# Diagonal recurrence of a third mixer: states in pairs, outputs in fours, small products alternating between row and column groups

## The chip, the cores and the metric

The kernel runs on one core of one Trainium2 chip. TensorE (PE) multiplies matrices, VectorE (DVE) and ScalarE (ACT) work elementwise, GpSimd (POOL) does almost nothing here, and the queue of SyncE (SP) issues the transfers from the chip's memory. All engines run their own instruction lists in order and wait for each other by semaphores. The metric is the time of one execution on the device in microseconds (us); the kernel before was timed three times.

## The reference: what is computed

A stack of layers over 256 tokens of width 1024: two blocks (a state space scan with neighbourhood attention, then an mLSTM, each with a feed-forward part) and then a third block. The third block's mixer adds up three branches of width 512: a gated attention ("fox"), a diagonal complex recurrence (S5), and a gated linear recurrence (HGRN2). Behind it come attention over a memory and a gated feed-forward part. The change touches the S5 branch alone:

```
def s5_mixer(u, a_re, a_im, b_re, b_im, c_re, c_im, d_skip, log_dt, w_glu, b_glu):
    ug = uf.reshape(bsz, seq, S5_GROUPS, S5_GROUP)
...
    drive_r = jnp.einsum('bsgh,gph->bsgp', ug, bbar_r)
    drive_i = jnp.einsum('bsgh,gph->bsgp', ug, bbar_i)
...
    _, _, h_r, h_i = lax.associative_scan(_complex_linear_combine, elems, axis=1)
    y = (jnp.einsum('bsgp,ghp->bsgh', h_r, c_re.astype(f32))
         - jnp.einsum('bsgp,ghp->bsgh', h_i, c_im.astype(f32)))
    y = y.reshape(bsz, seq, S5_W) + d_skip.astype(f32) * uf
    z = jax.nn.gelu(y)
    out = z * jax.nn.sigmoid(z @ w_glu.astype(f32) + b_glu.astype(f32))
```

## The kernel before, in words

The program is one long list of large products on PE. A weight unit (128 x 2048 numbers, `unit`, transfer at L437) is taken in two halves of 128 x 1024; ACT copies each half to its high part `wh` (L350) and DVE subtracts to get the low part `wl` (L359), and PE makes three products for each piece of weight (high by high, high by low, low by high; below: full products, 128 x 128 by 128 x 256 tokens). A unit is 48 of them. `wh` and `wl` have four buffers each, the raw weights three. The large sums lie in PSUM banks of the pool `mm`, the small ones in banks of the pool `ax`.

The third mixer (phase "mixer2") goes through its projections in the order `M2_ORDER = "su fox hz hv g2 g0 b0 glu dr g1 b1 b2"`. `su` makes the S5 input (two tiles `su` of 128 channels x 2 x 256 tokens) and then puts the generator `s5()` (L1357) into a list of background work. Between the units of large products the program calls `tick`, which takes a step or so of the other chains (fox, HGRN2) and of the background. A scheduler may then still move instructions within each engine.

The 2048 complex states are 16 blocks j of 128, and each block belongs to 32 of the 512 channels. One step of `s5()` handles one block: it loads a table of cosines and sines (`s5tl`), makes two drives on PE (`ax<-su,s5bt`: 32 rows of channels, from row 32 (j mod 4), to 128 states by 256 tokens, real and imaginary part into one `ax` bank), and then ten DVE instructions turn the drive by the table (two products, two half-sized sums), scan the two parts over the tokens with the state's magnitude, and turn back (two products). The work tiles are `s5w1` and `s5w2`; the trace shows both as `s5w`. One step later, by `lagged`, four products (`ax<-s5w,s5c`: 128 states to 32 partitions, from partition 32 (j mod 4), by 256 tokens) give the block's output; after each fourth block a DVE instruction adds the sum to `su`. These small products are in full float32, and the trace lists each as two passes (two rows each).

When all blocks are done, `s5()` ends with the gelu of `su`, and the unit `glu` multiplies it by its weights (`s5_gate`).

Of the kernel before, what the change touches and what calls it, by code (L numbers as in the profile page):

```python
# [19 lines left out]
P = 128  # L20
# [6 lines left out]
# order of the steps of the first mixer (x, z, q/k/v of attention; b: further background) and of the third one  # L27
# [3 lines left out]
# heads of the memory's keys and values that are projected at the ends of the layers' parts  # L31
FILLERS = [("k0 k1", "mm"), ("v0 v1", "ax"), ("k2 k3", "mm"), ("v2 v3", "ax")]
# units of the gated feed-forward that are computed by tokens first, and how many of them wait for their transposes
# [12 lines left out]
# ---------------------------------------------------------------- layout of the inputs  # L46
# [33 lines left out]
# the projections of the third mixer: name, first column, number of columns  # L80
# [11 lines left out]
def _units(w):  # L92
    """[1024, 256 m] -> m units [128, 8 * 256]"""
    m = w.shape[1] // T
    return w.reshape(8, P, m, T).transpose(2, 1, 0, 3).reshape(m, P, 2048)


def _down(w):
    """[256 m, 1024] -> m units [128, 2 * 1024]"""
    m = w.shape[0] // T  # L100
    return w.reshape(m, 2, P, D).transpose(0, 2, 1, 3).reshape(m, P, 2048)


def _square(w):
    """[512, 512 m] -> m units [128, 4 * 512]"""
    m = w.shape[1] // 512
    return w.reshape(4, P, m, 512).transpose(2, 1, 0, 3).reshape(m, P, 2048)
# [13 lines left out]
def prepare(i):  # L121
# [114 lines left out]
    # neighbourhood bias: entry (row distance, column distance), NEG outside of the window  # L236
# [29 lines left out]
# ---------------------------------------------------------------- the program  # L266

class Stack:
# [31 lines left out]
    # ---- small helpers  # L300
# [5 lines left out]
    def phase(self, name, mm=4, apart=(), swap=False):  # L306
        """tiles that live within one phase of the program; mm of the eight banks are for the large products;
        apart: tags with pools of their own, so that they lie where the neighbouring phases leave room in time"""
# [65 lines left out]
    # ---- steps of a chain that are put between the units of the large products  # L374
# [3 lines left out]
    def tick(self, n=1, background=1):  # L378
        """n steps of the chains in order (a chain that yields True waits for others), some of the background's
        (fractions add up)"""  # L380
# [22 lines left out]
    def held(self, on=True):  # L403
        """what is traced here is issued after the norm that ended the last phase"""
# [5 lines left out]
    def lagged(self, steps):  # L410
        """generator: each step's second part after the next one's first part"""
# [17 lines left out]
    # ---- weights: a unit is [128, 2048], taken as high and low parts in two halves  # L429
# [24 lines left out]
    def small_unit(self, name):  # L454
        """generator: a few columns for all inputs, in pieces of 512 of a tile's columns"""
# [11 lines left out]
    def proj_tok(self, u, xh, xl, kind="mm", after=False):  # L467
        """256 columns of x @ W -> [128 tokens, 2, 256]; after: behind the last phase's products, returns also
        the last product"""
# [12 lines left out]
    def proj_feat(self, u, xh, xl):  # L482
        """256 columns of x @ W -> [128 features, 2, 256 tokens]"""
# [11 lines left out]
    def proj_blocks(self, units, rows):  # L495
        """generator: as proj_feat for some units and proj_rows for one small one (rows: name, PSUM), two blocks of 128
        inputs at a time; the sums of one bank are one group, opened by the first product"""
# [24 lines left out]
    def proj_half(self, u, yh, yl):  # L522
        """512 columns of y [512 features] @ W -> two tiles [128 features, 2, 256 tokens]"""
# [14 lines left out]
    def down(self, units, acc, first, last):  # L538
        """acc[t][c] += y @ W with 256 rows of W each (units: (u, yh, yl), y [128, 2, 256]), one half
        of the tokens after the other"""  # L540
# [15 lines left out]
    def out_units(self, name, ys, order, tick=0, tail=2, early=0):  # L556
        """accumulators of y @ W; ys[j] is filled by the chains"""
# [23 lines left out]
    # ---- 1/sqrt(v*inv + eps) to float32 accuracy: a first guess from the exponent, then a  # L581
    # polynomial in v*guess^2 (its leading coefficient folded into the scale of v)
# [19 lines left out]
    # ---- split of a float32 value into two float32r parts (src may be in PSUM)  # L602
# [4 lines left out]
    def first_norm(self):  # L607
        """generator: rms norm of x, transposed, and the modulation of the first mixer (shift and scale), two
        blocks of 128 features at a time; scaled and shifted -> self.xh, self.xl"""
# [54 lines left out]
    def rms(self, x, xn):  # L664
        """1 / root mean square of the rows of x (xn: room for the squares)"""
# [39 lines left out]
    # ---- modulation: sums over the 1024 inputs of silu(c) * ada_w  # L705
# [9 lines left out]
    def cond_first(self, out):  # L715
        """silu(c) along the row on every partition, kept in DRAM"""
# [7 lines left out]
    def cond_row(self, out):  # L724
        """silu(c) along the row, on every partition"""
# [3 lines left out]
    def ada(self, layer, chunks, G=None, kind="ax"):  # L729
        """generator: a[.], b[.] columns of both norms and the rows of both gates"""  # L730
# [43 lines left out]
    # ---- x += G * rmsnorm(acc), or x += acc; then the norm of the next block  # L774
# [25 lines left out]
    # ---- layer 1 and 2: feed-forward  # L800
# [27 lines left out]
    # ---- softplus(v) and log_sigmoid(v)  # L828
# [12 lines left out]
    # ---- keys and values of the memory  # L841
    def mem_norm(self):
        """the normalised memory (features on partitions), kept in DRAM"""
# [17 lines left out]
    def mem_fill(self, what, kind, mh, ml):  # L861
        """keys (k) or values (v) of some heads, kept in DRAM, right behind the last phase's products; the first
# [494 lines left out]
    def s5(self, us):  # L1357
# [10 lines left out]
        def step(j):  # L1368
# [6 lines left out]
            for c in range(2):  # L1375
                self.matmul(dp[:, c], bt[b:b + 32, c, f], u[b:b + 32])
# [527 lines left out]
```

## Time and profile before

| | |
|---|---|
| time, median of 3 runs | 1548.85 us (1548.67 to 1549.3) |
| profiled execution, first to last instruction (span) | 1547.9 us; its time outside the span is not given |
| busy: PE, DVE, ACT, POOL | 96%, 75%, 55%, 0% of the span |
| mean granted clock of PE | 0.996 of full speed |
| third mixer's S5, first drive to the first product of `glu` | about 977.6 to 1194.9 us |

Busy shares are means over stages with different limits, so the stretch of S5 is read by itself. "Granted clock" is the share of full speed that the profile shows for PE in a stretch; 1.00 is 2.4 GHz and 0.50 is 1.2 GHz. The small products lie scattered among the large ones, so a reader looks for them by their tiles.

### The profile page before, as it was taken

How to read it: one execution, taken by the hardware profiler on the slowest of the kernel's cores; microseconds unless marked ns; L12 is line 12 of the kernel's file. 1: busy time of each engine (PE TensorE's matmuls, PEld its weight loads, DVE VectorE, ACT ScalarE, POOL GpSimd, SP SyncE). 2: the span in 40 equal slices, each digit the busy share in tenths (PEclk: the TensorE clock that was granted, in tenths of full speed). 3: DMA queues.
4: the chain of work that ended last, by engine and by line, in shares of the span. 5: the costliest groups of instructions: out<-in, count | busy, mean ns of one | idle time of the engine just before them, and what ended most of it. 6: DMA issues, size and time to landing. Idle time of an engine off the chain costs nothing.

```text
span 1547.9 us, 25416 instructions
## 1 busy us (share of the span) xinstructions
PE 1488.8 (96%) x9964; PEld 1325.5 (86%) x9964; DVE 1166.1 (75%) x2223; ACT 855.9 (55%) x1502; POOL 4.5 (0%) x26
## 2 busy tenths in 40 slices
PE   2899999999999989999999999999999999999999
PEld 2878887898898889998889989877789999799998
DVE  8788878877778896667988866858888987565555
ACT  4776765654546555554756765445444456454443
POOL 0000000000000000000000000000000000000000
PEclk9999999999999999999999999989999999999999
DMA  9656777577886785446576665323343355235552
GB/s 351 236 136 190 267 280 265 199 300 275 327 298 224 269 296 190 142 160 204 221 268 230 236 227 191 126 93 112 127 157 109 134 208 204 109 137 191 184 178 101
DMA packets 62058, 315.47 MB, mean 204 GB/s; under 512 B 6385, under 2 KB 15217, under 8 KB 28146
## 3 DMA queue, kind: packets, MB, share of 16 engines
q1 hardware_dynamic: 61938, 313.85, 57.5%
q8 instruction: 78, 1.28, 0.3%
q14 instruction: 42, 0.34, 0.1%
HBM read 304.77 MB, written 9.05 MB: 203 GB/s over the span
## 4 chain that ended last, share of the span: by engine, by line
PE 80%; DVE 11%; DMA 4%; ACT 3%; issue 2%; SPq 0%; ACTq 0%; DVEq 0%
PE mm L365 51%; PE ax L365 26%; DVE wl L359 2%; PE ax L369 2%; DMA bp<-cs_d 1%; DMA raw<-in_ada 1%; DVE acc L750 1%; ACT xn L350 1%; ACT wh L350 1%; DVE acc L637 1%; DMA bp<-nM_d 1%; DVE cva L362 0%; DVE qt L359 0%; DMA nb<-in_nab 0%; PE mm L369 0%
## 5 line engine op out<-in xcount | busy, mean ns | idle before, releaser
L359 DVE TENSOR_TENSOR wl<-raw,wh 128x1024 fp32r<-128x1024 f32 x400 | 485.5, 1222 | 202.2 <-ACT wh L350 201.6
L350 ACT ACTIVATE wh<-raw 128x1024 fp32r<-128x1024 f32 x400 | 419.5, 1057 | 369.3 <-PE mm L365 208.5
L365 PE MATMUL mm<-xh,wh 128*128 128x256 f32 x1536 | 441.3, 287 | 3.8 <-ACT bp L350 2.8
L365 PE MATMUL mm<-xh,wl 128*128 128x256 f32 x1536 | 439.3, 286 | 0.5 <-DVE wl L359 0.4
L365 PE MATMUL mm<-xl,wh 128*128 128x256 f32 x1536 | 439.4, 286 | 0.0
L365 PEld LDWEIGHTS mm<-xh,wh 128*128 128x128 f32 x1536 | 296.5, 193 | 13.8 <-issue 6.8
L365 PEld LDWEIGHTS mm<-xl,wh 128*128 128x128 f32 x1536 | 296.6, 193 | 7.8 <-issue 6.0
L365 PEld LDWEIGHTS mm<-xh,wl 128*128 128x128 f32 x1536 | 296.4, 193 | 5.3 <-issue 3.6
L365 PE MATMUL mm<-wh,xh 128*128 128x256 f32 x496 | 143.3, 289 | 0.0
L365 PE MATMUL mm<-wl,xh 128*128 128x256 f32 x496 | 141.8, 286 | 0.3 <-DVE wl L359 0.2
L365 PE MATMUL mm<-wh,xl 128*128 128x256 f32 x496 | 141.2, 285 | 0.0
L365 PE MATMUL ax<-wh,mhh 128*128 128x512 f32 x256 | 102.4, 400 | 0.0
L365 PE MATMUL ax<-wl,mhh 128*128 128x512 f32 x256 | 101.3, 396 | 0.0
L365 PE MATMUL ax<-wh,mhl 128*128 128x512 f32 x256 | 101.3, 396 | 0.0
L365 PEld LDWEIGHTS mm<-wl,xh 128*128 128x128 f32 x496 | 94.9, 191 | 3.4 <-issue 2.3
L365 PEld LDWEIGHTS mm<-wh,xh 128*128 128x128 f32 x496 | 94.8, 191 | 3.0 <-issue 2.5
L365 PEld LDWEIGHTS mm<-wh,xl 128*128 128x128 f32 x496 | 94.9, 191 | 1.6 <-issue 1.5
L365 PEld LDWEIGHTS ax<-wh,mhl 128*128 128x128 f32 x256 | 48.1, 188 | 12.0 <-DVE mhl L359 0.4
L365 PEld LDWEIGHTS ax<-wh,mhh 128*128 128x128 f32 x256 | 48.2, 188 | 10.7 <-ACT wh L350 0.5
L365 PEld LDWEIGHTS ax<-wl,mhh 128*128 128x128 f32 x256 | 48.1, 188 | 10.7 <-issue 0.5
L362 DVE SCALAR_TENSOR_TENSOR acc<-raw,cond,acc 128x1024 f32<-128x1024 f32 x28 | 35.8, 1278 | 9.3 <-DMA raw<-in_ada 9.1
L750 DVE CUSTOM_DVE_ANT_0 acc<-raw,crow 128x1024 f32<-128x1024 f32 x32 | 39.0, 1219 | 2.4 <-DMA raw<-in_ada 2.1
(486 smaller groups left out, 2601.4 us busy)
## 6 DMA issues: line engine op xcount, KB each, us to landing
raw<-in_wts SPq DMA_DIRECT2D x214, 1024.0 KB, 4.9
raw<-in_ada SPq DMA_DIRECT2D x48, 1024.0 KB, 6.0
nb<-in_nab SPq DMA_DIRECT2D x16, 256.0 KB, 2.9
grow<-in_rows SPq DMA_DIRECT2D x16, 256.0 KB, 5.1
bp<-cs_d SPq DMA_DIRECT2D x16, 256.0 KB, 6.2
s5tab<-s5t SPq DMA_DIRECT2D x16, 256.0 KB, 2.5
s5tl<-s5tab SPq DMA_DIRECT2D x16, 256.0 KB, 2.9
meml<-mem_d SPq DMA_DIRECT2D x2, 1024.0 KB, 6.2
```

Of the source, the lines that this page charges most:

```text
L350: return self.nc.scalar.activation(out=out, in_=in_, func=func, **kw)
L359: return self.nc.vector.tensor_tensor(out=out, in0=in0, in1=in1, op=op)
L362: return self.nc.vector.scalar_tensor_tensor(out=out, in0=in0, scalar=s, in1=in1, op0=op0, op1=op1)
L365: return self.nc.tensor.matmul(out, lhsT, rhs, start=start, stop=stop)
L369: return self.nc.tensor.transpose(out, in_, self.ident[0:k, 0:k])
L637: nc.vector.tensor_tensor_reduce(out=acc, in0=raw[:, k * D:(k + 1) * D], in1=self.crow, scale=1.0, scalar=0.0, op0=ALU.mult, op1=ALU.add, ...
L750: nc.vector.tensor_tensor_reduce(out=acc, in0=w, in1=self.crow, scale=1.0, scalar=0.0, op0=ALU.mult, op1=ALU.add, accum_out=s8[:, j:j + 1])
```

## The change

`s5()` now takes the blocks in pairs. A step p loads two tables, takes two `ax` banks, and issues the four drives of its two blocks so that neighbouring products use different groups of 32 rows (block 2p+1, then 2p, for the real part, and again for the imaginary part). The DVE work of both blocks follows, with the same ten instructions for each. After every second pair, `outputs(f)` makes all sixteen output products of four blocks at once, in an order where neighbouring products write different groups of 32 partitions. A helper `after` adds dependencies of issue order alone, so that all of a group come behind its first. The first work tile of a block now lies in the space of `merged0` to `merged3` (each used later for the merged branches), the second in four buffers of `s5w2`; the gelu uses `s5w2` too. The pool `mm` has four of the eight PSUM banks in this phase instead of five, `ax` four instead of three. The rest of the diff (left out here) removes comments.

```
+    def after(self, first, later):
+        if first is None:
+            return later
+        self.order(later, first)
+        return first
...
-        def step(j):
-            b, f = 32 * (j % 4), j // 4
+        held = []
+
+        def step(p):
+            f = p // 2
             u = us[f // 2][:, f % 2]
-            tab = self.pt("s5tl", [P, 2, T], bufs=2)
-            nc.sync.dma_start(out=tab, in_=self.s5tab[j].rearrange("p (a b) -> p a b", a=2))
-            co, si = tab[:, 0], tab[:, 1]
-            dp = self.ax((P, 2, T))
+            js = (2 * p, 2 * p + 1)
+            tabs, dps = [], []
+            for j in js:
+                tab = self.pt("s5tl", [P, 2, T], bufs=2)
+                nc.sync.dma_start(out=tab, in_=self.s5tab[j].rearrange("p (a b) -> p a b", a=2))
+                tabs.append(tab)
+                dps.append(self.ax((P, 2, T)))
+            first = None
             for c in range(2):
-                self.matmul(dp[:, c], bt[b:b + 32, c, f], u[b:b + 32])
-            w1 = self.pt("s5w1", [P, 2, T], bufs=2)
-            w2 = self.pt("s5w2", [P, 2, T], bufs=2)
...
-            def rest():
-                if j % 4 == 0:
-                    yps.append(self.ax((P, 512))[:, 0:T])
-                yp = yps[-1]
-                # C_re (re cos - im sin) - C_im (re sin + im cos)
-                for i, (c, w) in enumerate(((0, w2[:, 0]), (2, w1[:, 1]), (1, w1[:, 0]), (1, w2[:, 1]))):
-                    self.matmul(yp[b:b + 32], cc[:, c, j], w, i == 0, i == 3)
-                if j % 4 == 3:
-                    self.stt(u, u, self.col("s5d", f), yp, ALU.mult, ALU.add)
-            return rest
-
-        yield from self.lagged([partial(step, j) for j in range(16)])
+                for j, dp in zip(js[::-1], dps[::-1]):
+                    b = 32 * (j % 4)
+                    first = self.after(first, self.matmul(dp[:, c], bt[b:b + 32, c, f], u[b:b + 32]))
+            for j, tab, dp in zip(js, tabs, dps):
+                w1 = self.pt(f"merged{j % 4}", [P, 2, T])
+                w2 = self.pt("s5w2", [P, 2, T], bufs=4)
...
+                held.append((j, w1, w2))
+
+        def outputs(f):
+            u = us[f // 2][:, f % 2]
+            yp = self.ax((P, 512))[:, 0:T]
+            first = None
+            for i in range(4):
+                for j, w1, w2 in held[::-1]:
+                    b = 32 * (j % 4)
+                    c, w = ((0, w2[:, 0]), (2, w1[:, 1]), (1, w1[:, 0]), (1, w2[:, 1]))[i]
+                    first = self.after(first, self.matmul(yp[b:b + 32], cc[:, c, j], w, i == 0, i == 3))
+            held.clear()
+            self.stt(u, u, self.col("s5d", f), yp, ALU.mult, ALU.add)
+
+        for p in range(8):
+            step(p)
+            yield
+            if p % 2:
+                outputs(p // 2)
+            yield
...
-            a = self.pt("s5w1" if i == 0 else "s5w2", [P, 2, T], bufs=2)
+            a = self.pt("s5w2", [P, 2, T], bufs=4)
...
-    with S.phase("mixer2", 5, LATE2):
+    with S.phase("mixer2", 4, LATE2):
```

What follows shows the order of instructions on two engines; the numbers behind the names tell apart the tiles of one tag. On PE before, near the end of S5, the drives of block 15 and the outputs of block 14 stand together between two full products (`mm`):

```order
L365 MATMUL mm_12284<-xh_9998,wl_12292 128x256
L365 MATMUL ax_12347<-su1_10393,s5bt_10561 128x256 x2
L365 MATMUL ax_12192<-s5w2_12271,s5c_10563 32x256
L365 MATMUL ax_12192<-s5w1_12270,s5c_10563 32x256 x2
L365 MATMUL ax_12192<-s5w2_12271,s5c_10563 32x256
L365 MATMUL mm_12364<-xh_9998,wh_12367 128x256
```

The same engine after the change has the four drives of a pair (p = 6, blocks 12 and 13) between two full products:

```order
L365 MATMUL mm_12015<-xh_9998,wl_12023 128x256
L365 MATMUL ax_12102<-su1_10393,s5bt_10561 128x256
L365 MATMUL ax_12099<-su1_10393,s5bt_10561 128x256
L365 MATMUL ax_12102<-su1_10393,s5bt_10561 128x256
L365 MATMUL ax_12099<-su1_10393,s5bt_10561 128x256
L365 MATMUL mm_12127<-xh_9998,wh_12130 128x256
```

And the last outputs of the changed kernel, `outputs(3)`, stand on PE with blocks 15, 14, 13 and 12 in turn (the first eight of sixteen products, and the full product ahead of them):

```order
L365 MATMUL mm_12369<-xl_9999,wh_12372 128x256
L365 MATMUL ax_12351<-s5w2_12281,s5c_10563 32x256
L365 MATMUL ax_12351<-s5w2_12271,s5c_10563 32x256
L365 MATMUL ax_12351<-s5w2_12118,s5c_10563 32x256
L365 MATMUL ax_12351<-s5w2_12108,s5c_10563 32x256
L365 MATMUL ax_12351<-merged3_12280,s5c_10563 32x256
L365 MATMUL ax_12351<-merged2_12270,s5c_10563 32x256
L365 MATMUL ax_12351<-merged1_12117,s5c_10563 32x256
L365 MATMUL ax_12351<-merged0_12107,s5c_10563 32x256
```

Two products that stood next to each other before used the same rows and columns of the array; now neighbours differ in them. In the changed order the drives stand in 12 runs (five pairs whole, p = 2 and 5 broken up by products of fox, p = 7 in two halves with 34 full products between them), and the sixteen outputs of the four calls in 8 (one whole, two broken once, one twice). Between the last drives of a pair and the outputs that need it stand, on PE: 111 full products and then the transposes of `qksq` (p = 1), 72 full products (p = 3), 64 (p = 5), and 64 to the first product that needs the split described next (p = 7).

On DVE before, at the end of S5, the work on block 14 is mixed with splits of weights (`wl`):

```order
L359 TENSOR_TENSOR wl_12368<-raw_12365,wh_12367 128x1024
L359 TENSOR_TENSOR s5w1_12270<-ax_12267,s5tl_12265 128x512
L359 TENSOR_TENSOR s5w2_12271<-ax_12267,s5tl_12265 128x512
L359 TENSOR_TENSOR wl_12372<-raw_12365,wh_12371 128x1024
L359 TENSOR_TENSOR s5w1_12270<-s5w1_12270,s5w2_12271 128x256 x2
L372 SCALAR_TENSOR_TENSOR s5w2_12271<-mag_8452,s5w1_12270 128x256 x2
L359 TENSOR_TENSOR s5w1_12270<-s5w2_12271,s5tl_12265 128x512
L359 TENSOR_TENSOR s5w2_12271<-s5w2_12271,s5tl_12265 128x512
L359 TENSOR_TENSOR wl_12446<-raw_12443,wh_12445 128x1024
```

After the change, blocks 14 and 15 (p = 7) stand there interleaved, behind three splits in a row, and the split `wl_12377` of a unit still to be multiplied comes behind most of them:

```order
L359 TENSOR_TENSOR merged2_12270<-ax_12262,s5tl_12260 128x512
L359 TENSOR_TENSOR s5w2_12271<-ax_12262,s5tl_12260 128x512
L359 TENSOR_TENSOR merged3_12280<-ax_12265,s5tl_12263 128x512
L359 TENSOR_TENSOR merged2_12270<-merged2_12270,s5w2_12271 128x256 x2
L359 TENSOR_TENSOR s5w2_12281<-ax_12265,s5tl_12263 128x512
L372 SCALAR_TENSOR_TENSOR s5w2_12271<-mag_8452,merged2_12270 128x256 x2
L359 TENSOR_TENSOR merged3_12280<-merged3_12280,s5w2_12281 128x256
L359 TENSOR_TENSOR merged2_12270<-s5w2_12271,s5tl_12260 128x512
L359 TENSOR_TENSOR merged3_12280<-merged3_12280,s5w2_12281 128x256
L359 TENSOR_TENSOR s5w2_12271<-s5w2_12271,s5tl_12260 128x512
L372 SCALAR_TENSOR_TENSOR s5w2_12281<-mag_8452,merged3_12280 128x256 x2
L359 TENSOR_TENSOR wl_12377<-raw_12370,wh_12376 128x1024
```

Where before one split stood between pieces of a single block's chain, now a chain of two blocks stands ahead of it.

## Rows read from the trace of the kernel before

**Rows 1.** The page: busy time of each engine; the chain that ended last.

```profile
PE 1488.8 (96%) x9964; PEld 1325.5 (86%) x9964; DVE 1166.1 (75%) x2223; ACT 855.9 (55%) x1502; POOL 4.5 (0%) x26
...
PE 80%; DVE 11%; DMA 4%; ACT 3%; issue 2%; SPq 0%; ACTq 0%; DVEq 0%
```

**Rows 2.** What PE waited for, 950 to 1250: us in total, times, longest.

```profile
PE ax L365 <- DVE s5w L359: 0.2, 1, 0.2
```

**Rows 3.** S5's stretch: us, busy (x) of PE, PEld, DVE, ACT, POOL; PEclk, DMA, GB/s.

```profile
978.70:1194.90 216.20, 215.00 (x1408) 173.90 (x1408) 170.81 (x324) 95.20 (x159) 1.08 (x2) 0.98 0.34 116
```

**Rows 4.** Passes and loads by tile: ns least/median/most, first and last start, shapes.

```profile
L365 PE MATMUL ax<-su,s5bt x64: 374/374/478, 977.6 to 1162.3; 32*128 32x256 f32 x64
...
L365 PEld LDWEIGHTS ax<-s5w,s5c x128: 106/110/110, 989.9 to 1181.0; 128*32 128x32 f32 x128
L365 PE MATMUL ax<-s5w,s5c x128: 379/379/404, 989.9 to 1181.3; 128*32 128x256 f32 x128
```

**Rows 5.** Timeline of PE around one block: start, duration, instruction.

```profile
1161.35 0.28 PE L365 MATMUL mm<-xh,wl 128*128 128x256 f32 x1
1161.56 1.12 PE L365 MATMUL ax<-su,s5bt 32*128 32x256 f32 x4
1162.61 1.91 PE L365 MATMUL ax<-s5w,s5c 128*32 128x256 f32 x8
1164.46 0.39 PE L365 MATMUL mm<-xh,wh 128*128 128x256 f32 x1
1164.68 0.28 PE L365 MATMUL mm<-xl,wh 128*128 128x256 f32 x1
```

**Rows 6.** Timeline of PE, three places with small products of different row or column groups.

```profile
95.08 1.14 PE L365 MATMUL ax<-nk,nq 64*128 64x256 f32 x8
...
108.89 1.09 PE L365 MATMUL ax<-qt,xt 128*64 128x256 f32 x8
...
1016.61 0.48 PE L365 MATMUL ax<-fr,cst 32*128 32x256 f32 x1
1016.61 0.48 PE L365 MATMUL ax<-su,s5bt 32*128 32x256 f32 x1
1016.92 0.37 PE L365 MATMUL ax<-fr,cst 32*128 32x256 f32 x1
```

**Rows 7.** DVE's groups, 975 to 1195: busy us, mean ns | idle before.

```profile
L359 DVE TENSOR_TENSOR wl<-raw,wh 128x1024 fp32r<-128x1024 f32 x43 | 52.2, 1219 | 9.4 <-ACT wh L350 9.4
...
L359 DVE TENSOR_TENSOR s5w<-ax,s5tl 128x512 f32<-128x512 f32 x32 | 20.8, 684 | 7.6 <-PE ax L365 7.5
L372 DVE TENSOR_TENSOR_SCAN s5w<-mag,s5w 128x256 f32<-128x256 f32 x32 | 20.3, 675 | 0.1
```

**Rows 8.** Timeline of DVE within one block: start, duration, instruction.

```profile
1137.13 1.28 DVE L359 TENSOR_TENSOR s5w<-ax,s5tl 128x512 f32<-128x512 f32 x2
1138.33 0.47 DVE L362 SCALAR_TENSOR_TENSOR su<-su,cols,ax 128x256 f32<-128x256 f32 x1
1138.72 0.75 DVE L359 TENSOR_TENSOR s5w<-s5w,s5w 128x256 f32<-128x256 f32 x2
1139.39 1.22 DVE L359 TENSOR_TENSOR wl<-raw,wh 128x1024 fp32r<-128x1024 f32 x1
1140.53 1.27 DVE L372 TENSOR_TENSOR_SCAN s5w<-mag,s5w 128x256 f32<-128x256 f32 x2
1141.71 0.67 DVE L359 TENSOR_TENSOR xn<-hb,hz 128x512 f32<-128x512 f32 x1
```

**Rows 9.** As rows 3, over the stretch with the low clock.

```profile
1014.00:1030.00 16.00, 16.00 (x70) 12.08 (x71) 8.84 (x24) 8.23 (x18) 0.00 (x0) 0.68 0.17 55
1018.00:1026.00 8.00, 8.00 (x27) 6.02 (x28) 6.29 (x19) 5.22 (x10) 0.00 (x0) 0.50 0.01 2
```

**Rows 10.** The tile `qksq`, 999 to 1012: first and last reader of one `mm` bank.

```profile
L350 ACT ACTIVATE qksq<-mm x1: 597/597/597, 1000.4 to 1000.4; 128x512 f32<-128x512 f32 x1
...
L359 DVE TENSOR_TENSOR qksq<-mm,qkr4r x1: 692/692/692, 1010.7 to 1010.7; 128x512 f32<-128x512 f32 x1
```

More of the change, by code (lines that the diff above doesn't have):

```diff
@@ L1365, in s5 @@
         self.act(cc[:, 1], cc[:, 1], scale=-1.0)
-        yps = []
-        def step(j):
-            b, f = 32 * (j % 4), j // 4
+        held = []
+        def step(p):
+            f = p // 2
             u = us[f // 2][:, f % 2]
-            tab = self.pt("s5tl", [P, 2, T], bufs=2)
-            nc.sync.dma_start(out=tab, in_=self.s5tab[j].rearrange("p (a b) -> p a b", a=2))
-            co, si = tab[:, 0], tab[:, 1]
-            dp = self.ax((P, 2, T))
-            for c in range(2):
-                self.matmul(dp[:, c], bt[b:b + 32, c, f], u[b:b + 32])
-            w1 = self.pt("s5w1", [P, 2, T], bufs=2)
-            w2 = self.pt("s5w2", [P, 2, T], bufs=2)
-            cob = co.unsqueeze(1).to_broadcast([P, 2, T])
-            sib = si.unsqueeze(1).to_broadcast([P, 2, T])
-            self.tt(w1, dp, cob, ALU.mult)
-            self.tt(w2, dp, sib, ALU.mult)
-            self.tt(w1[:, 0], w1[:, 0], w2[:, 1], ALU.add)
-            self.tt(w1[:, 1], w1[:, 1], w2[:, 0], ALU.subtract)
-            mg = self.mag[:, j:j + 1].to_broadcast([P, T])
-            for c in range(2):
-                self.scan(w2[:, c], mg, w1[:, c], 0.0, ALU.mult, ALU.add)
-            self.tt(w1, w2, sib, ALU.mult)
-            self.tt(w2, w2, cob, ALU.mult)
-            def rest():
-                if j % 4 == 0:
-                    yps.append(self.ax((P, 512))[:, 0:T])
-                yp = yps[-1]
-                for i, (c, w) in enumerate(((0, w2[:, 0]), (2, w1[:, 1]), (1, w1[:, 0]), (1, w2[:, 1]))):
-                    self.matmul(yp[b:b + 32], cc[:, c, j], w, i == 0, i == 3)
-                if j % 4 == 3:
-                    self.stt(u, u, self.col("s5d", f), yp, ALU.mult, ALU.add)
-            return rest
@@ new lines, in step @@
+            for j, tab, dp in zip(js, tabs, dps):
+                w1 = self.pt(f"merged{j % 4}", [P, 2, T])
+                w2 = self.pt("s5w2", [P, 2, T], bufs=4)
+                cob = tab[:, 0].unsqueeze(1).to_broadcast([P, 2, T])
+                sib = tab[:, 1].unsqueeze(1).to_broadcast([P, 2, T])
+                self.tt(w1, dp, cob, ALU.mult)
+                self.tt(w2, dp, sib, ALU.mult)
+                self.tt(w1[:, 0], w1[:, 0], w2[:, 1], ALU.add)
+                self.tt(w1[:, 1], w1[:, 1], w2[:, 0], ALU.subtract)
+                mg = self.mag[:, j:j + 1].to_broadcast([P, T])
+                for c in range(2):
+                    self.scan(w2[:, c], mg, w1[:, c], 0.0, ALU.mult, ALU.add)
+                self.tt(w1, w2, sib, ALU.mult)
+                self.tt(w2, w2, cob, ALU.mult)
+                held.append((j, w1, w2))
```

## The prediction

> **What bounds the kernel now.** I read the page first. PE is busy in 96% of the span, and 80% of the chain that ended last is PE's [rows 1]: time is won where PE's work gets shorter or a wait of PE goes. Then I asked what PE waited for in the third mixer. In 300 us around S5 it waited for a block's DVE work (`s5w`) once, for 0.2 us [rows 2]. So S5 costs time through PE's own slots, and DVE's chain is hidden behind the large products. But not with much to spare: in S5's stretch of 216.2 us DVE is busy for 170.8 us, 79% [rows 3]. The reader should keep both in mind, because the change shortens PE's share and leaves DVE's as it is.
>
> Next the price of a block on PE. The stretch has 64 passes of drives and 128 of outputs, with 374 and 379 ns from start to end [rows 4]; they are pipelined, so durations can't be added up. The timeline gives slots [rows 5]: the eight output passes last 1.91 us, so a slot is (1.91 - 0.379)/7 = 0.22 us. The last full product before starts at 1161.35 and keeps its slot of 0.12 us, to 1161.47. Behind the block one full product starts at 1164.46 and the next at 1164.68, where their usual distance is the 0.12 slot; so the array is given back at 1164.68 - 0.12 = 1164.56. A block takes 3.09 us. Twelve slots of 0.22 are 2.64, and the other 0.45 us goes into three changes: full to drives, drives to outputs, outputs to full. A run of drives or of outputs alone has two of the three, 0.30; I take 0.33, a little more, since the change to and from full products may be the dearer one.
>
> **PE's sum before.** 192 passes x 0.22 = 42.2 us. In the order before, six blocks stand as in [rows 5] (6 x 0.45 = 2.7) and the other drives and outputs form 23 separate runs (23 x 0.33 = 7.6). Together 52.5 us.
>
> **PE's sum after.** The same 192 passes are issued, with neighbours on different groups of 32 rows or columns. Do such passes run side by side? The trace has the nearest cases [rows 6]. Eight passes of two heads on 64 rows each take 1.14 us including the last one's tail, so a pass costs (1.14 - 0.37)/7 = 0.11, half a slot. Eight passes on two groups of 64 columns, into one bank, take 1.09, the same. And a drive of S5 with another product of 32 rows: both start at 1016.61, the next pass at 1016.92. So two groups share a slot, for rows and for columns. Four groups of columns are in no row. The bounds: four share one slot (0.055 a pass), or only two do (0.11), or none (0.22). I take the first, since two rows each show the whole array filled by what fits on it.
>
> Outputs: 128 passes / 4 = 32 slots. Drives: five whole pairs and the split one have 8 passes on two groups, 4 slots each, 24; p = 2, broken up, 8; p = 5, 6; together 38. 70 slots x 0.22 = 15.4. The runs are now 20 (8 and 12, counted in the order): 20 x 0.33 = 6.6. Sum 22.0; **saved 30.5 us**. With two columns at a time it is 32 slots more (7.0 us less saved), with none 96 more (21.1 less).
>
> Here a rule bears on it that no row shows. The Trainium skill, "TensorE: Matmul & The Clock Gate", Part 3 (packing small matmuls), gives a measured speedup of 3.07 for four row tiles and 2.38 for three column tiles, and says that weight loads overlap with running matmuls only when the row group differs. By 3.07 the outputs would take 28.2/3.07 = 9.2 us and not 7.0 (an estimate), 2.2 us less saved; by its rule on loads, column groups would lie nearer to the middle bound.
>
> **What DVE gives back.** Its instructions are the same ten for each block. Starts in [rows 8] lie apart by 0.60 (full products), 0.335 (half sums), 1.14 (a split) and 0.59 (scans), a little under the durations of [rows 7] since neighbours overlap. A pair has 8 products, 4 half sums and 4 scans: 4.8 + 1.34 + 2.36 = 8.5 us. Before, the output of a block had a whole step to wait in; now sixteen outputs wait for the last block of a pair, and large products behind them on PE wait too. What stands between decides, at 0.12 us for a full product:
> p = 1: 111 products, 13.3 us. DVE has the pair (8.5), five splits (5.7) and about 2.2 of small work, 16.4, of which 1.8 start earlier than the count on PE: 1.3 to 1.7 late; I take 1.7, with the transposes behind it.
> p = 3: 72 products, 8.6 us, against the pair and small work: 0.5 late.
> p = 5: 64 products, 7.7 us, against 8.5 + 0.7: 1.5 late.
> p = 7: 64 products to the one that needs `wl_12377`, 7.7 us. Ahead of that split DVE has three splits (3.4), most of the pair (7.4) and the split itself (1.1), 11.9, of which 1.5 lie before the drives: 2.7 late. The splits behind it are late in turn, and the last outputs: 1.5.
> Sum 7.9 us. Bounds: nothing, if DVE gets ahead by starting each pair earlier; and on the other side DVE's idle time. It was 216.2 - 170.8 = 45.4 us of the stretch. With 30.5 - 7.9 = 22.6 us gone, 22.8 of it are left, half, and the stretch is 193.6 us. If three quarters must stay, because splits wait for ACT (9.4) and blocks for their drives (7.6) as before [rows 7], 11.4 are gained.
>
> **Costed at nothing.** The pool `mm` loses a bank. The longest hold that I found is the 10.3 us from the first to the last reader of a `qksq` bank [rows 10]; three other banks give three units of 48 products, 17 us. If that cover went, a unit would wait at most the difference, about a microsecond at the ends. Table loads are as many as before, and a pair's two lie two steps ahead. The dependencies of issue order cost no instruction. The tiles in `merged0` to `merged3` are free until the branches are merged, behind S5.
>
> **The clock.** In 16 us around 1022 PE's granted clock is 0.68, with 0.50 (1.2 GHz) from 1018 to 1026, where few products ran [rows 9]: 16 x 0.32 = 5.1 us lost. The changed order has the same thin mixture of small products there. I leave one such fall in the sum; none or two would move it by 5.1.
>
> **Sum.** 30.5 - 7.9 = 22.6 us. The profiled span of 1547.9 becomes 1525.3, and the median of 1548.85, 0.95 above it, 1526.
>
> **Rivals.**
> B. Columns pass only two at a time. [Rows 6] show two and no more, and an output's load of weights takes 0.110 us [rows 4]: if the loads of four column groups go one behind the other, a pass costs 0.11 however many groups there are. (The rule on loads of the Trainium skill, cited above, speaks for this.) PE saves 23.5; a later PE meets less waiting for DVE, about 2 of the 7.9: 1548.85 - 23.5 + 5.9 = 1531.
> C. DVE becomes the bound. For it: 79% busy, and 88% in a stretch of 193.6 us, with pairs in lumps of 8.5 us ahead of splits. Gain 11.4: 1537.5. Against it: the few waits walked above are short and lie apart.
> D. It doesn't do what it says: passes of 32 columns don't overlap and the pairs hardly, since each pass must wait for its own weights. Then only switches go (52.5 - 42.2 - 6.6 = 3.7), and waits of a few microseconds eat it: 1548. Against it, [rows 6].
> E. Slower: each change of group costs what a change between full and small products does. The 96 small products would make about 96 changes where 29 runs stood before. At 0.33 that is 31.7 + 42.2 = 73.9 against 52.5, 21.4 us more: 1570. It decides from (52.5 - 42.2 + 3.1)/96 = 0.14 us a change. Against it: passes of two groups that start in the same instant [rows 6].
>
> **How the numbers follow.** Main case 0.53 (1526, its own range 1517 to 1535: no wait at all, or twice the waits, with the clock's 5 us partly in it). B 0.20, C 0.14, D 0.07, E 0.06. The range 1517 to 1541 takes in the first three and leaves out D, E and a little at its lower end. About 0.2%, 3 us, is what a measurement here can tell from no change: faster 0.87 (main, B and C), same 0.07 (D), slower 0.06 (E).
>
> **What the profile after would show.** Right: the output passes of a whole run start four at a time about 0.22 apart, so that `outputs(3)` takes some 2.1 us and not 7; drives of a pair start in twos; the stretch from the first drive to `glu` is about 194 us; waits of PE for `s5w2`, `merged` and `wl` appear, 2 to 3 us at p = 7, some 8 in all; DVE is busy 88% of the stretch. B: starts two at a time, 4 us for sixteen outputs. C: waits over 15 us in all, or gaps at many splits. D: starts one at a time. E: gaps within a run. It would be wrong by something I didn't price if PE's waits name an `mm` bank, a table or a `merged` tile, or if the clock falls at other places.

## The result, and the profile after

| | before | changed |
|---|---|---|
| median | 1549.3 us (1548.67 to 1553.59, 5 runs) | 1537.69 us (1533.04 to 1542.84, 5 runs) |
| span of the profiled execution | 1547.9 us | 1534.2 us |
| mean granted clock in it | 0.996 | 0.987 |

The ratio is 0.9913, with a 95% interval of 0.9884 to 0.9942: 13.5 us faster, 9 to 18 (the two medians differ by 11.6). Two later measurements of the same changed kernel on other chips gave 0.9889 (0.9865 to 0.9913) and 0.9876 (0.9845 to 0.9906), 17 and 19 us. The forecast was 22.6, a time of 1526: the first measurement lies in the stated range of 1517 to 1541, but above the main case's own, 1517 to 1535, which the two later ones meet (1531.4 and 1531.17).

The page of the changed kernel, its busy times and the chain that ended last by engine, answers to [rows 1]:

```profile
PE 1466.6 (96%) x9964; PEld 1317.4 (86%) x9964; DVE 1163.1 (76%) x2223; ACT 857.0 (56%) x1502; POOL 4.5 (0%) x26
...
PE 68%; DVE 16%; DMA 8%; ACT 5%; issue 3%; SPq 0%; ACTq 0%; DVEq 0%
```

PE is 22.2 us less busy with the same 9964 instructions, and of the chain that ended last DVE now holds 16% instead of 11%. The stretch of S5, from the first drive to the first product of `glu`, answers to [rows 3] (columns as there; the kernel before first, the changed one below):

```profile
977.60:1194.90 217.30, 216.10 (x1413) 174.57 (x1412) 171.91 (x324) 96.04 (x161) 1.08 (x2) 0.98 0.34 118
...
982.40:1180.20 197.80, 188.68 (x1413) 161.84 (x1412) 170.60 (x326) 97.58 (x162) 1.08 (x2) 0.97 0.38 130
```

The stretch before was 217.3 us; it is 19.5 us shorter, and DVE is busy for 86% of it. Note where the stretch begins: 4.8 us later than before, although S5's new order begins only there. The span alone hides this. What the sixteen last outputs do shows on PE's timeline, and answers to [rows 5]:

```profile
1152.20 0.28 PE L365 MATMUL mm<-xl,wh 128*128 128x256 f32 x1
1152.41 0.64 PE L365 MATMUL ax<-s5w,s5c 128*32 128x256 f32 x8
1152.87 1.05 PE L365 MATMUL ax<-merged,s5c 128*32 128x256 f32 x16
1153.73 0.61 PE L365 MATMUL ax<-s5w,s5c 128*32 128x256 f32 x8
1154.28 0.39 PE L365 MATMUL mm<-xh,wl 128*128 128x256 f32 x1
```

Eight passes stand at 1152.41, the next sixteen at 1152.87: the 32 passes take 1.87 us, so four groups of columns share each slot of 0.22. The whole drives of a pair, eight passes, take 1.07:

```profile
1079.69 1.13 PE L365 MATMUL ax<-su,s5bt 32*128 32x256 f32 x8
1080.76 0.39 PE L365 MATMUL mm<-wh,xh 128*128 128x256 f32 x1
```

What PE waited for from 970 to 1200 (us in total, times, longest) answers to [rows 2]; before, the list over that stretch came to 1.6 us, and here it comes to 9.6:

```profile
PE mm L365 <- DVE wl L359: 3.3, 2, 2.5
PE ax L369 <- DVE qt L355: 2.9, 2, 2.3
PE ax L369 <- DVE qksq L359: 1.7, 3, 1.1
PE mm L365 <- DVE merged L362: 0.9, 1, 0.9
PE ax L369 <- DVE qkr4v L356: 0.8, 1, 0.8
```

The fourth line is no wait for a work tile of S5, although those lie in `merged` too. PE's product reads `fyh` and `wh`, and DVE's instruction reads an `mm` bank, so PE must be waiting for that bank to be read:

```profile
1170.75 0.69 DVE L362 SCALAR_TENSOR_TENSOR merged<-fx,mm 128x512 f32<-128x512 f32 x1
...
1171.50 0.39 PE L365 MATMUL mm<-fyh,wh 128*128 128x256 f32 x1 [0.88 <-DVE merged L362]
```

The two longest, on PE's timeline (in brackets the wait and who ended it):

```profile
1132.11 0.70 PE L365 MATMUL ax<-su,s5bt 32*128 32x256 f32 x4
1135.29 0.56 PE L365 MATMUL mm<-xh,wl 128*128 128x256 f32 x1 [2.48 <-DVE wl L359]
...
1045.79 0.30 PE L369 MATMUL ax<-cst,qt 128*128 128x128 f32 x1 [2.32 <-DVE qt L355]
```

Which pair does the first of these wait for? The drives ahead of it on PE are the first half of p = 7. But DVE's first instruction on a block reads both parts of its drives, and the second half of p = 7 comes at 1141. The chain on DVE that holds back the split starts at 1126.77: it is that of p = 6.

```profile
1126.77 0.67 DVE L359 TENSOR_TENSOR merged<-ax,s5tl 128x512 f32<-128x512 f32 x1
...
1134.03 1.20 DVE L359 TENSOR_TENSOR wl<-raw,wh 128x1024 fp32r<-128x1024 f32 x1
...
1141.89 0.69 DVE L359 TENSOR_TENSOR merged<-ax,s5tl 128x512 f32<-128x512 f32 x1
...
1149.18 1.21 DVE L359 TENSOR_TENSOR wl<-raw,wh 128x1024 fp32r<-128x1024 f32 x1
```

The split behind the chain of p = 7, for which the prediction had 2 to 3 us, is the one at 1149.18, and PE waits 0.81 us for it:

```profile
1150.44 0.38 PE L365 MATMUL mm<-xh,wl 128*128 128x256 f32 x1 [0.81 <-DVE wl L359]
```

And the windows behind the two longest waits: PE's granted clock is 0.50, that is 1.2 GHz, within about a microsecond after each.

```profile
1047.00:1056.00 9.00, 9.00 (x32) 5.93 (x31) 6.46 (x14) 2.61 (x8) 0.00 (x0) 0.50 0.45 147
...
1135.30:1138.70 3.40, 3.40 (x16) 3.40 (x17) 3.40 (x5) 0.00 (x0) 0.00 (x0) 0.51 0.63 234
```

The first fall lasts 10.2 us, like the one before the change [rows 9], and the second 3.4.

### The profile page after: what moved, and what is told of

The parts are those of the page before. It is cut to its first block, busy times and chain, and to the rows that moved or that the text cites. A ratio compares the mean times of both kernels' runs of the same rounds, so it can differ in the third digit from the quotient of the medians.

```text
span 1534.2 us, 25399 instructions
## 1 busy us (share of the span) xinstructions
PE 1466.6 (96%) x9964; PEld 1317.4 (86%) x9964; DVE 1163.1 (76%) x2223; ACT 857.0 (56%) x1502; POOL 4.5 (0%) x26
## 4 chain that ended last, share of the span: by engine, by line
PE 68%; DVE 16%; DMA 8%; ACT 5%; issue 3%; SPq 0%; ACTq 0%; DVEq 0%
PE mm L365 45%; PE ax L365 21%; DVE wl L359 4%; DMA raw<-in_ada 2%; PE ax L369 2%; ACT wh L350 1%; DMA bp<-cs_d 1%; DMA raw<-in_wts 1%; DMA grow<-in_rows 1%; DVE merged L359 1%; ACT xn L350 1%; DVE s5w L372 1%; DVE s5w L359 1%; DVE acc L637 1%; DMA bp<-nM_d 1%
## 5 line engine op out<-in xcount | busy, mean ns | idle before, releaser
L362 DVE SCALAR_TENSOR_TENSOR acc<-raw,cond,acc 128x1024 f32<-128x1024 f32 x28 | 35.8, 1279 | 10.6 <-DMA raw<-in_ada 10.4
```

The costliest lines, as they stand in the source:

```text
L362: return self.nc.vector.scalar_tensor_tensor(out=out, in0=in0, scalar=s, in1=in1, op0=op0, op1=op1)
```

## The experiments

Twelve runs were made in three groups, each group on one chip. The stretch of S5 says more than the time, since the time also holds falls of the clock elsewhere; ratios are to the kernel before on the same chip.

**1. The changed kernel again, twice, and the kernel before again** (no edits).

> The changed kernel once more, nothing edited. The first profile of it has a S5 stretch (first drive to first product of glu) of 197.7 us against 217.3 before, 19.6 less, but a span only 13.7 us less, since its clock was at 0.50 for some 24 us within its first 105 us, before anything that was changed. Theory: those early falls belong to the single execution, not to the change. Then the stretch is again 196 to 199 us, the time lies anywhere from 1529 to 1543, and executions of the kernel before on this chip show such falls too (spreads of several us, mean clocks under 0.996). Rival: the changed program causes them; then this profile shows them again at the same places and the kernel before is steady at 1549.

> The changed kernel once more on one chip with the version with single drives. Theory: its stretch is again 196 to 200 us, with the waits of 2.5 us near its 61st and 2.6 us near its 150th us each followed within 3.5 us by a fall of the clock to 0.50 (3.4 to 10.2 us long). Rival: the falls lie elsewhere or are missing while the waits are there.

> The kernel before once more, nothing edited, for a second trace of it. Theory: the early falls of the clock (10.2 us at 34, 3.4 at 47, 3.4 at 68, 3.4 to 6.8 at 95 us), which every kernel run later has and its first trace has not, belong to the execution; they show here too, and S5's stretch is again 217 us within 3, with one fall of the clock in it. Rival: they come with the changed program; then none is here.

Measured: the changed kernel 1531.4 us and 1531.17 us (ratios above); its stretch 197.8 and 193.2 us. The kernel before 1550.38 us, ratio 0.9995 (0.9977 to 1.0014), stretch 216.0. The early falls are there in all three. From 33 to 45 us the kernel before has, in its second trace:

```profile
33.00:45.00 12.00, 9.05 (x62) 8.85 (x61) 9.69 (x20) 5.21 (x9) 0.00 (x0) 0.84 1.01 393
```

and the changed kernel, in its first:

```profile
33.00:45.00 12.00, 8.86 (x63) 8.66 (x62) 9.69 (x20) 5.30 (x9) 0.00 (x0) 0.86 0.98 388
```

So such falls come without the change too; the trace of experiment 6 has them as well. (On the profile's time the falls that the expectation lists begin 11 us earlier, at 23, 36, 57 and 84 us; the window holds the one at 36.) All ten traces with the changed S5 have those at 23 and 36 us, and of the four without it two, its first trace being one of the others: whether the changed program makes them likelier, so few traces can't tell. They are at most a part of why its first span fell by 13.7 us only: with them the kernel before begins S5 at 975.3 us, without them at 977.6. Over all traces S5 begins at 975.3 to 980.3 us without the change and at 975.6 to 985.7 with it. Behind S5, from the first product of `glu` to the end, the changed kernel takes 353.4 to 354.0 us, the kernel before 352.9 and 353.0.

In S5 the traces differ by the falls. The second trace has the first one's (10.2 and 3.4 us). The third has 3.4 us at 1033 and 3.4 behind the wait for `wl`:

```profile
1128.24 0.39 PE L365 MATMUL mm<-xh,wl 128*128 128x256 f32 x1 [2.48 <-DVE wl L359]
...
1128.82 0.41 PE L365 MATMUL mm<-xh,wh 128*128 128x256 f32 x1
```

(0.41 is a full product at 1.2 GHz; 0.28 is its usual duration). There the wait for `qt` was 0.8 us instead of 2.3, and no fall followed. The expectations that the stretch is 196 to 200 us and that both waits and both falls come back were wrong for this one: PE, slowed by 1.7 us at 1033, met DVE's work 1.5 us later, and the wait shrank by as much.

**2. Outputs in the order of the blocks.**

```
-            for i in range(4):
-                for j, w1, w2 in held[::-1]:
+            for (j, w1, w2), i in [(h, i) for h in held[::-1] for i in range(4)]:
```

with dependencies of order that keep the list so.

> The sixteen outputs of a call in the order of the blocks (four products of block 15, then four of 14, and so on) instead of alternating; everything else as changed. Theory A (groups of columns share a slot only where neighbours in the list alternate): a call takes 32 slots of 0.22, about 7 us, instead of 1.9, 4 x 5.2 = 21 us more on PE, of which up to 8 replace waits for DVE: 12 to 21 us slower than the changed kernel, about 1550. Rival B (it is enough that the products stand together; the array looks ahead past a product whose columns are busy): a call stays near 1.9 us and the time within 3 us of the changed kernel. In between, if it looks ahead a few passes: 3 to 5 us a call.

Measured: 1543.08 us, ratio 0.9959 (0.9941 to 0.9976), 11.7 us above the changed kernel on that chip; stretch 206.3. Neither A nor B, but the case in between, 3 to 5 us a call: the four blocks run two at a time. The last outputs on PE:

```profile
1156.59 0.62 PE L365 MATMUL ax<-s5w,s5c 128*32 128x256 f32 x2
1157.05 0.81 PE L365 MATMUL ax<-merged,s5c 128*32 128x256 f32 x3
1157.49 0.40 PE L365 MATMUL ax<-s5w,s5c 128*32 128x256 f32 x1
1157.70 0.38 PE L365 MATMUL ax<-merged,s5c 128*32 128x256 f32 x1
1157.73 0.56 PE L365 MATMUL ax<-s5w,s5c 128*32 128x256 f32 x2
...
1160.59 0.59 PE L365 MATMUL ax<-s5w,s5c 128*32 128x256 f32 x2
1161.12 0.39 PE L365 MATMUL mm<-xh,wl 128*128 128x256 f32 x1
```

A block's list is `s5w`, `merged`, `merged`, `s5w`, two passes each. The pass of `s5w` at 1157.49 stands among the first block's four of `merged`, and must be the next block's first product, which the list has behind the first block's fourth. So PE starts passes ahead of earlier ones in the list whose columns are busy, but it doesn't reach far enough to fill four groups. (That engines run their lists in order, as the words ahead of the prediction have it, is not true of these passes.) 4.53 us instead of 1.87, four times, is 10.6 us (the other three calls are broken up by other products, and taken as equal), and the time rose by 11.7.

**3. Drives in the order of the blocks.**

```
-            for c in range(2):
-                for j, dp in zip(js[::-1], dps[::-1]):
+            for j, dp in zip(js[::-1], dps[::-1]):
+                for c in range(2):
```

> The four drives of a pair in the order of the blocks (both parts of block 2p+1, then both of 2p); everything else as changed. Theory: products of two heads that stand as A, A, B, B in the list (queries and keys of the second mixer) already run side by side in the trace, so a whole pair of drives still takes 1.06 us and the time is that of the changed kernel within 2 us. Rival: without alternation the pair takes 8 slots, 1.9 us, 0.9 more in six places: 5 us slower less what waits absorb, 3 to 5 us.

Measured: 1537.08 us, ratio 0.9911 (0.9888 to 0.9935), 5.7 us above the changed kernel, which looks like the rival. The trace says otherwise. (The products of two heads that the expectation speaks of, the first of [rows 6], belong to the first mixer.) A whole pair takes 1.07 us as ever:

```profile
1080.24 1.14 PE L365 MATMUL ax<-su,s5bt 32*128 32x256 f32 x8
1081.31 0.38 PE L365 MATMUL mm<-wh,xh 128*128 128x256 f32 x1
```

The stretch is 205.7 us, since this execution's clock was low for 30.7 us where the others had 3.4 to 10.2:

```profile
1013.00:1044.00 31.00, 31.00 (x112) 18.84 (x112) 10.51 (x29) 14.97 (x31) 0.00 (x0) 0.51 0.15 56
```

That is 10.2 us more lost in that fall than in one of 10.2. With falls and waits taken off, PE's slots save 29.1 us here, as in the changed kernel (the table below). The time is the clock's too. The record has the mean clock of every execution; the time multiplied by one minus that clock, an estimate of what low clock costs, is 20.5 us on average here and 16.6 for the changed kernel on that chip, and the mean times differ by 3.5. For the drives alternation is worth nothing; whether this order tends to the longer fall, six executions can't tell.

**4. Outputs one step later.**

```
         for p in range(8):
+            if p and p % 2 == 0:
+                outputs(p // 2 - 1)
             step(p)
             yield
-            if p % 2:
-                outputs(p // 2)
             yield
+        outputs(3)
```

> The outputs of four blocks one step of the background later, together with the next pair's drives; everything else as changed. Theory: about 9.5 of the 30 us that PE saves is lost to waits for DVE, because the outputs and the splits behind a pair come too early; with more products between, the waits of 1.3 us at the first outputs, 0.8 before the third and part of the 2.6 us behind the last pair go: 2 to 5 us faster than the changed kernel, a stretch of 193 to 196 us. Rival: the waits only move (the next pair on DVE starts later, behind the outputs, and the splits behind it are late): within 2 us, or up to 3 us slower.

Measured: 1528.49 us, ratio 0.9861 (0.984 to 0.9882), 2.9 us below the changed kernel, but the two intervals overlap; stretch 191.6. The waits for `wl` are gone, and the list comes to 7.0 us instead of 9.6. Two waits grew: that for the `mm` bank's reader (`merged`) from 0.9 to 1.6, and that for `qt` from 2.3 to 2.9. The clock did not fall behind the latter. It had been low for 10.2 us from 1019.7 on, among small products and without such a wait:

```profile
1048.52 0.30 PE L369 MATMUL ax<-cst,qt 128*128 128x128 f32 x1 [2.92 <-DVE qt L355]
1048.58 0.36 PE L365 MATMUL mm<-xh,wh 128*128 128x256 f32 x1
```

**5. Less work for DVE, after and before.** In both kernels the two last products of each block are left out, so that the outputs are not the reference's:

```
-                self.tt(w1, w2, sib, ALU.mult)
-                self.tt(w2, w2, cob, ALU.mult)
```

> The changed kernel without the last two DVE products of each block (the turning back by sine and cosine is left out, so that the outputs are made of the scans and of the sums before them): 2.4 us less DVE work for each pair, 19 us in all; PE's list keeps its products. Theory: the 9.4 us of new waits of PE (1.3, 2.5, 0.8, 2.6, 1.0, 1.0 us at six places) are DVE's, so most of them go: 5 to 9 us faster than the changed kernel, 24 to 27 us below the kernel before, a stretch of S5 of 189 to 193 us. Rival: the waits have another cause (ACT, banks, the order of the list): time and stretch within 3 us of the changed kernel (stretch 197.7).

> The kernel before without the last two DVE products of each block (left out as in the light version of the changed kernel, 19 us less DVE work). Theory: before the change DVE's chain was hidden, PE waited 0.2 us for it; nothing is won, within 3 us of the kernel before, so that the 10 us which the same cut gives the changed kernel are all waits that the change made. Rival: DVE's work costs PE time there as well (through splits or the clock): 5 to 10 us faster.

Measured: the changed kernel 1521.88 us, ratio 0.9815 (0.9787 to 0.9843), a stretch of 186.1 without a fall of the clock; the kernel before 1548.01, ratio 0.9978 (0.9962 to 0.9994), a stretch of 213.3. By the ratios, and across chips, the cut is worth 9 to 15 us after the change, more than the 5 to 9 of the theory. Before the change it is worth 3.4 us (0.9 to 5.9), between theory and rival; the stretch is 4.0 us shorter there, 3.4 of them from a shorter fall of the clock (3.4 us long instead of 10.2). So the change made DVE count. Of PE's two largest waits in the changed kernel the one for `wl` is gone, and of the one for `qt` 0.8 us are left:

```profile
PE ax L369 <- DVE qksq L359: 2.0, 4, 1.2
PE ax L369 <- DVE fr L372: 1.3, 1, 1.3
PE ax L369 <- DVE qt L355: 1.1, 2, 0.8
PE ax L365 <- DVE s5w L372: 1.0, 1, 1.0
```

**6. The banks alone**, the kernel before with `S.phase("mixer2", 4, LATE2)`.

> The kernel before with only the banks changed: four banks for the large sums in the third mixer and four for the small ones. Theory: nothing waits for a bank there; within 1.5 us of the kernel before, no wait of PE for a reader of an mm bank over 0.5 us. Rival: a part of the expected gain was lost to the missing bank; then 3 us or more slower.

Measured: 1548.91 us, ratio 0.9989 (0.9972 to 1.0006). One wait for a bank's reader is new, behind S5 (950 to 1250, columns as above):

```profile
PE mm L365 <- DVE fx L362: 0.8, 1, 0.8
```

The changed kernel has the same wait, the kernel before has none over that ground. So the missing bank costs 0.8 us there, which is behind S5, more than the 0.5 that was expected of any one wait, and nothing that the time can tell. The prediction had priced it at about a microsecond at the ends if the cover went.

**7. DVE's work on the second block one step later.**

```
             for j, tab, dp in zip(js, tabs, dps):
+                if j % 2:
+                    yield
```

and the outputs as in 4.

> Drives in pairs as in the changed kernel, but DVE's work on the second block of a pair comes one background step later, and the outputs one step after it, together with the next pair's drives. PE's sum is that of the late outputs (some 22 us). Theory: the waits come from lumps of 8.5 us of DVE work ahead of small steps of the other chains; with lumps of 4.2 us the waits of 1.3, 3.1 and 1.7 us that the late outputs still had shrink: 1 to 4 us faster than the late outputs, 22 to 26 us below the kernel before. Rival: the sum of DVE's work in the stretch decides, not its lumps: within 1.5 us of the late outputs.

Measured: 1529.64 us, ratio 0.9856 (0.9828 to 0.9884), the same as 4; stretch 195.4, with 17.1 us of low clock in it against 10.2 in 4. The waits moved and did not go, 8.7 us in all against 7.0:

```profile
PE mm L365 <- DVE merged L362: 2.9, 1, 2.9
PE mm L365 <- DVE wl L359: 2.4, 2, 1.4
```

The rival's number came: shorter lumps alone win nothing. That the sum of DVE's work decides is not shown by it.

**8. Outputs in fours, drives singly.** Each call of `outputs` comes one step later as well, as in 4, so this is not one part of the changed kernel alone:

```
-            js = (2 * p, 2 * p + 1)
...
+        for j in range(16):
+            if j and j % 4 == 0:
+                outputs(j // 4 - 1)
+            step(j)
+            yield
+        outputs(3)
```

> One part alone: outputs in fours, but the drives of one block at a time in sixteen steps (with the next block's drives behind the outputs). On PE the drives take 64 slots instead of 38 and four or five runs more: 26 x 0.22 + 5 x 0.33 = 7.4 us more than the changed kernel. DVE's lumps are half as long, so that waits of 9.4 us shrink to 3 or 4. Theory: 0 to 4 us slower than the changed kernel, some 14 to 18 us below the kernel before; outputs alone carry two thirds of the gain or more. Rival: pairing the drives is what pays: within 8 us of the kernel before.

> The version with single drives and outputs in fours once more, on one chip with the changed kernel. Theory: 7.4 us more slots of PE, but the waits for DVE (9.4 to about 3 us) and the falls of the clock behind them (5 to 7 us) gone: 3 to 7 us faster than the changed kernel, and a stretch of 190 us within 2. Rival: the difference seen so far is that of two chips; then within 2 us of the changed kernel.

Measured: 1528.02 and 1525.53 us, ratios 0.9848 (0.9824 to 0.9872) and 0.9831 (0.9803 to 0.9859), on one chip 5.6 us below the changed kernel (the intervals overlap slightly); stretches 190.1 twice. The first expectation had the sign wrong, the second held. It has the lowest time of those that compute all of the reference; from the paired drives with late outputs of 4 (ratio 0.9861) the intervals don't part it. By the estimate of experiment 3 low clock cost it 11.6 us and the changed kernel on that chip 17.9, which is the whole difference. Its stretch and what PE waited for in it:

```profile
983.70:1173.80 190.10, 187.28 (x1413) 161.48 (x1413) 171.39 (x324) 96.83 (x161) 1.08 (x2) 1.00 0.40 134
```

```profile
PE mm L365 <- DVE merged L362: 0.9, 1, 0.9
PE ax L369 <- DVE fr L372: 0.9, 1, 0.9
PE ax L365 <- ACT qt L350: 0.8, 1, 0.8
PE ax L369 <- DVE qksq L359: 0.5, 2, 0.3
PE ax L369 <- DVE qkr4w L359: 0.2, 1, 0.2
```

The clock is 1.00 throughout the stretch.

## Why the prediction was right, point by point

How the gain comes about was forecast rightly: PE saves slots, and waits for DVE take a part of them back. The largest term, PE's slots, was right in kind and size; the waits were right only in their sum, and the clock's term was too small.

The stretches can be put together from three parts. To the difference from the stretch before (217.3 us, with 10.2 us of low clock and 1.6 us of listed waits) are added half of the low clock that a trace has more, and the waits that it has more; the sum is an estimate of what PE's own slots saved.

| kernel | stretch | low clock in it | waits | saved by PE |
|---|---|---|---|---|
| changed, first | 197.8 | 13.6 | 9.6 | 19.5 + 1.7 + 8.0 = 29.2 |
| changed, second | 197.8 | 13.6 | 9.8 | 19.5 + 1.7 + 8.2 = 29.4 |
| changed, third | 193.2 | 6.8 | 8.1 | 24.1 - 1.7 + 6.5 = 28.9 |
| outputs in blocks | 206.3 | 6.8 | 10.9 | 11.0 - 1.7 + 9.3 = 18.6 |
| drives in blocks | 205.7 | 34.1 | 7.1 | 11.6 + 12.0 + 5.5 = 29.1 |
| outputs later | 191.6 | 10.2 | 7.0 | 25.7 + 0 + 5.4 = 31.1 |
| second block later | 195.4 | 17.1 | 8.7 | 21.9 + 3.4 + 7.1 = 32.4 |
| less work for DVE | 186.1 | 0 | 5.4 | 31.2 - 5.1 + 3.8 = 29.9 |
| drives singly | 190.1 | 0 | 3.3 | 27.2 - 5.1 + 1.7 = 23.8 |

**PE's sum.** 30.5 us were forecast and 29 were saved. The step taken without a row, that four groups of columns share one slot, is right: 1.87 us for sixteen outputs, where some 2.1 had been named with the change behind them. One behind the other, 32 slots would take 7.04 us, 3.8 times as long. The price of singles (7.4 us) measured 29.2 - 23.8 = 5.4, or 31.1 - 23.8 = 7.3 against the paired drives with late outputs, whose calls of `outputs` stand as in the kernel with singles. The Trainium skill, "TensorE: Matmul & The Clock Gate", Part 3, measured a speedup of 2.38 for three column tiles and 3.07 for four row tiles (the prediction's estimate of 9.2 us applied the latter to columns); here four column groups came to that 3.8, and the measurement decides. The same part of the Trainium skill says that loads of weights overlap with running products only where the row group differs; here all outputs use the same 128 rows, and at four passes a slot of 0.22 us the loads of 0.110 us each [rows 4] are hidden all the same.

**Waits.** 7.9 us forecast, 8.0 added by the list: that the sum fits is luck. At the places that the prediction walked, some 3.4 us came. The first outputs: 1.7 against 1.1. p = 3: 0.5 against nothing. The third outputs: 1.5 against 0.6, for `qt`. p = 7: 2.7 against 0.8. The tail: 1.5 against the 0.9 for the bank's reader. The other 4.8 us came at two pairs that it did not walk, since no outputs stand behind them: 2.3 us for `qt` at p = 2, in two traces of three, a step of fox behind a pair's work on DVE; and 2.5 us for the split behind the work of p = 6. I had walked only the outputs and the splits behind the last pair.

**The bank.** "Costed at nothing" was wrong by 0.8 us behind S5. The 0.9 us for a bank's reader within S5 came with DVE's work late and with four banks. Less work for DVE removes it, and four banks alone don't make it; the changed kernel with five banks was not run. Waits that name an `mm` bank were among the prediction's signs of something not priced, and so this was. (A wait for a `merged` tile stands in the prediction both as a sign of being right and as one of being wrong.)

**The clock.** "I leave one such fall in the sum" failed in all three traces: a second fall of 3.4 us came behind the wait for the split of p = 6. The low clock in S5 lasted 13.6, 13.6 and 6.8 us and not 10.2. In the first two traces the longer fall, too, came behind a wait, the one for `qt`, and not in the thin mixture of small products where it was expected.

**The time.** By stretch the gain is 19.5 to 24.1 us around the forecast of 22.6 (1.3 less against the second trace of the kernel before, 216.0); by time it measured 13.5, 17 and 19. Most of what lies between is low clock over the whole execution. By the estimate of experiment 3 it cost the changed kernel 23.1 us in the first measurement, where two of five executions lay above 1541, and 16.6 and 17.9 in the two later ones. On the chips of those two it cost the kernel before 12.7 and 11.7. Time multiplied by mean clock fell from 1537.3 to 1516.0 us and from 1540.2 to 1515.3, 21 and 25, which is the forecast. So the term that was too small is the clock: the forecast left the low clock as it was, and the changed kernel had some 4 to 6 us more of it.

**Rivals.** The time alone could not have told the cases apart: the first measurement, 1537.69, meets rival C's 1537.5, and the two later ones meet rival B's 1531. The traces decide. B is out for the changed order, with 1.87 us a call, and is nearly what the order by blocks gives (4.53). C is half right: DVE did become what PE waits for, as the two light kernels show, but with 9.6 us of waits and not over 15, and 27.2 us of DVE's idle time are left in the first trace, 22.9 in the third, where 22.8 had been the main case's. (That three quarters of it must stay was an assumption: the two waits named for it come to 17.0 of 45.4 us.) D and E are out by the same 1.87 us.

## What to carry to other kernels

Small products that use 32 of the 128 columns run side by side, four in a slot, if the list brings the groups close together; for 32 rows two in a slot were seen, since no more stood together. With eight passes of one group in a row PE reaches ahead, but fills only half. When products that waited harmlessly among others are gathered, the saved slots come off the cover of the other engine's chain. Here paired drives saved 5 to 7 us of slots more than single ones and gave them back in waits and low clock: the kernel with single drives and late outputs was at least as fast. Look for waits behind every gathered lump, and not only where its results are read. Compare stretches and clocks before medians; a fall of the clock can be larger than the effect of an edit.

## What the runs showed that was not expected

In S5, waits of PE of over 2 us came with the lower clock nearly every time. Five were for the split at the first drives of p = 7 (2.1 to 2.5 us, in five traces), and about when each ended the clock fell for 3.4 us. Of five others of 2.3 to 2.9 us four were like that, with falls of 3.4 to 10.2 us, and the one of 2.9 us before `qt` in experiment 4 was not. So such a wait can cost its length and 1.7 to 5.1 us more. That the wait is the cause is inferred from the order of events, and it is no rule: in the first trace of the kernel before, waits of 2.1, 2.5 and 3.2 us near 70, 83 and 544 us were followed by no fall, and in experiment 7 one of 1.4 us at 1052 was. Nor does a fall need such a wait: all four traces without the change have one of 3.4 to 10.2 us in S5, among small products. Of the versions with the changed S5, the two without such waits (less work for DVE in 5, and 8) had no fall there.
